# First weight pieces one k-tile at a time, seven warming products, and three reorderings in the DeltaNet stage of a two-layer decoder trunk

## The chip, the cores and the metric

The kernel runs on one core of one Trainium2 chip. The metric is the device time of one execution in microseconds. Engines are named as in the profile: PE is TensorE (PEld its weight loads), DVE is VectorE, ACT is ScalarE, POOL is GpSimd and SP is SyncE, which issues most DMAs.

## The reference, cut to what matters

The computation is a two-layer decoder trunk over 512 positions and a model width of 1024. Layer 0 mixes tokens by a gated DeltaNet with 8 heads of width 128, layer 1 by a Conformer convolution. Both layers then cross-attend into 256 memory rows and apply a squared-ReLU MLP of width 4096.

```python
h = x
for layer in range(DEPTH):
    if layer % N_MIXERS == 0:
        h = h + gated_deltanet(rms_norm(h, dn_norm[j]), dn_w_in[j], ...)
    else:
        h = h + conformer_conv(rms_norm(h, cv_norm[j]), ...)
    h = h + memory_cross_attention(rms_norm(h, xa_norm[layer]), rms_norm(mem, ...), ...)
    h = h + sq_relu_mlp(rms_norm(h, mlp_norm[layer]), mlp_w_up[layer], mlp_w_down[layer])
return rms_norm(h, final_norm)
```

The change lies in the first half of layer 0. There the input is projected to q, k, v, z and to two gate values per head; q, k and v pass a causal convolution of width 4 and a SiLU; and the delta rule is solved in chunks, which needs the inverse of a triangular matrix for each head and chunk:

```python
beta = jax.nn.sigmoid(b_raw)
g = -jnp.exp(a_log) * jax.nn.softplus(a_raw + dt_bias)
...
a_mat = jnp.eye(DN_CHUNK, dtype=q.dtype) + lower
sol = lax.linalg.triangular_solve(a_mat, rhs, left_side=True, lower=True, unit_diagonal=True)
...
return o.astype(h.dtype).reshape(B, S, DN_INNER) @ w_out
```

## The kernel before, in words

**Products.** Each fp32 product is made of three matmuls on split operands: a value is cut into a high part (`wh`, `xh`, an fp32r copy made by ACT) and a low part (`wl`, `xl`, the remainder, made by DVE), and `mm3` (L236 to L240) multiplies high by high, high weights by low input, and low weights by high input into one PSUM bank. Weights come in pieces of 128x1024 (eight k-tiles of 128x128, a "unit" of 24 matmuls): SP loads the raw piece, ACT casts it (`wh`, L214), DVE subtracts (`wl`, L69). Raw pieces, `wh` and `wl` have three buffers each, so that the cast of one unit waits for the end of the unit three before it.

**Order.** The work of the DeltaNet stage is a list `mains` of units of PE (the projections) and a table `S` of side jobs by unit, with ranks; `run` emits them in that order, and a scheduler then lays each engine's instructions out. An engine runs its own instructions strictly one after another. `tc.keep_in_program_order` holds the marked instructions in the order in which they are written.

**The start.** The first unit (`mm_ab`) multiplies the first k weights and, with the same input tiles, the gate columns (`ab`): five matmuls for each of eight k-tiles. For it the kernel loads eight tiles `x` of the input (256 KB each), the norm's gains `gn0`, the gate columns `wab` and the raw weights `raw0` in four pieces of two k-tiles (`piece`, L106). Piece 0 and 1 are issued on ACT's queue, the rest on SP's in the order x0, gn0, wab, x1, x2, piece 2, x3, x4, piece 3, x5 to x7. A loop (L1298 to L1308) splits the pieces and tiles in that order, pinned. Until the data are there, PE multiplies constants: `WARM` products of 128x128 (L125), each two records in the trace.

**The norm's spread.** The RMS norm's factor per token is computed beside the first units; `spread` (L355) makes it a row for all partitions by four PE transposes (`rb`, L308) and a copy on ACT. It stands after the first part of the third unit (`k`, 2), which `halves` cuts after two k-tiles. `gates` (L387) stands inside that unit's second part, after k-tile `CUT_G`: it transposes the gate values (`abT`, L391), and a series of small DVE operations (`sm`) makes `g` and `beta`. From `g` come `grep` (L431), a PE product `ct` (L454), its copy `gsum` on ACT (L456), and on DVE the matrices `R` and `L` (L69, L72), which the PE products `dt` (L475) multiply. PE's products `dt` stand right behind unit (`q`, 1) and three small products `gsum` (L469 to L471).

**The inverse.** `fs_steps` solves 32x32 blocks by 31 steps on DVE; `fs_end` transposes the result to `UB` (L601); `mg_a` (L613) copies the blocks of each head to `u0` (L617, two copies on ACT and two on DVE a head) and transposes it on DVE to `x0` (L619); `mg_w` multiplies `x0` on PE (`mg`, L628), heads 0 and 1 in one place of the order, heads 2 and 3 one unit later.

**The output.** `do_mm` (L1430) multiplies the heads' outputs `oh`, `ol` (made by `head_out`) with the output weights, in `mm3`'s order.

Of the kernel before, what the change touches and what calls it, by code (L numbers as in the profile page):

```python
# [14 lines left out]
P = 128  # L15
# [22 lines left out]
def tile_trunk(ctx, tc, xT, memT, x_d, mem_d, prm_d, adt_d, bdw_d, tap_d, fin_d, w_ab, w_kq, w_v, w_z, w_dno, w_pw1, w_pw2,  # L38
               w_q, w_k, w_vv, w_o, w_up, w_dn, yT):
    nc = tc.nc  # L40
# [64 lines left out]

    def piece(e, i):  # L106
        e.dma_start(out=raw0[:, i * 256:(i + 1) * 256], in_=w_kq[0][:, i * 256:(i + 1) * 256])

    piece(act, 0)
    wab = slot(s="wab")[:, 0:P]  # L110
    def load_first():
        nc.sync.dma_start(out=gn0, in_=prm_d[:, 0:8])
        nc.sync.dma_start(out=wab, in_=w_ab)

    xin = load_x({0: load_first, 2: lambda: piece(nc.sync, 2), 4: lambda: piece(nc.sync, 3)})
    adt = const([P, 16], "adt")

# [6 lines left out]
    for i in range(WARM):  # L124
# [6 lines left out]
                       base=0, channel_multiplier=1)  # L131
    piece(act, 1)
    ones_r = const([P, P], "ones_r", F32R)
# [235 lines left out]
    class DeltaNet:  # L369
# [243 lines left out]
        def mg_a(self, h):  # L613
            (u0, bt), n = self.M[h], slice(h % 4 * 4, h % 4 * 4 + 4)
            for b in range(4):
                bs = slice(32 * b, 32 * b + 32)
                (act.copy if b % 2 else dve.tensor_copy)(c4(u0)[bs, :, bs], self.fs[h // 4][bs, n, :])  # L617
            x0 = slot(s="x0")
            dve.transpose(out=x0, in_=u0)  # L619
            self.M[h] = u0, x0, bt  # L620
# [676 lines left out]
    pin = tc.keep_in_program_order  # L1297
    for i in range(4):  # L1298
        s = slice(i * 256, (i + 1) * 256)
        pin(act.copy(hl0[0][:, s], raw0[:, s]))  # L1300
        pin(tt(dve, hl0[1][:, s], raw0[:, s], hl0[0][:, s].bitcast(F32), ALU.subtract))
        for k in (2 * i, 2 * i + 1):
            n0.parts(k, xin[k], pin)
# [29 lines left out]
    def main(kind, h):  # L1333
        at[kind, h] = len(mains)
        k2 = (kind, h) == ("k", 2)
        mains.extend(halves((kind, h // 2), h % 2, n0.xs, D.ps, (kind, h), 2 if k2 else 4, {CUT_G: D.gates} if k2 else None))

# [92 lines left out]
    def do_mm(q, m):  # L1430
        if m % 2 == 0:
            wdo[0] = wnext(("do", 2 * q + m // 4), m // 2 % 2)
        ps = psum("do")
        for k in range(4):
            mm3(ps, wk(wdo[0], m % 2 * 4 + k), os_[4 * q + k], k == 0, k == 3)
        return ps
# [15 lines left out]
    h = []  # L1452
# [72 lines left out]
LAG = (0, 0, 1)  # L1525
WARM = 9
FENCE = 9
T_STAT = 5
CUT_G = 5
T_DEC = 13  # L1530
# [127 lines left out]
```

## Time and profile before

| what | value |
|---|---|
| median of 3 runs | 1502.61 us (1502.39 to 1503.71) |
| the profiled execution's own time | 1502.59 us |
| its span, first to last instruction | 1500.9 us |
| PE busy | 1492.3 us, 99% of the span |
| DVE, ACT, POOL busy | 894.5, 685.1, 211.7 us |
| granted TensorE clock | 1.0 |

The profiled execution lies 1.7 us above its span and within 0.1 us of the median. The profile's page gives the span, busy time by engine and the chain that ended last. The timeline view lists instructions in order of time: start in us, duration in us, engine, line, operation, output<-inputs, shapes, count, and in square brackets the engine's idle time before it with what ended it. The view of waits sums idle time by what ended it (total, times, longest). The windows view gives each engine's busy time in stretches of time. Matmuls are pipelined: a matmul of 512 columns is shown with 0.39 us, but the next one starts earlier than that.

### The profile page before, as it was taken

The numbers are of one execution on the slowest core, as the hardware profiler recorded it, in microseconds if no ns is written. First come the engines' busy times: TensorE is split into PE (matmuls) and PEld (weight loads), VectorE is DVE, ScalarE is ACT, GpSimd is POOL, SyncE is SP. The second block draws the span as 40 slices with busy tenths as digits, with TensorE's granted clock in tenths as the row PEclk, the third lists the DMA queues.
The fourth block names the chain that finished last, engine by engine and source line by source line (L and its number), as shares of the span: only waits on it lengthen the run. The fifth ranks groups of instructions, "written<-read, shape, count | busy, mean of one in ns | idle before, by whom it ended". The sixth has DMA issues, their size and how long they took to land.

```text
span 1500.9 us, 19206 instructions
## 1 busy us (share of the span) xinstructions
PE 1492.3 (99%) x7458; PEld 1257.9 (84%) x7458; DVE 894.5 (60%) x1318; ACT 685.1 (46%) x1202; POOL 211.7 (14%) x223
## 2 busy tenths in 40 slices
PE   9999999999999999999999999999999999999998
PEld 7888889888888888888888889988888888888886
DVE  6889888867555543444445799976555543434441
ACT  7856765555444432322324464564444431423332
POOL 1401310102111000000002496211111000000000
PEclk9999999999999999999999999999999999999999
DMA  7231223522212222223233624532122223322221
GB/s 250 74 119 57 71 85 113 182 85 88 81 47 95 99 98 98 98 99 97 92 126 128 190 87 138 173 123 98 57 71 91 92 98 98 98 98 99 98 99 56
DMA packets 50059, 155.65 MB, mean 104 GB/s; under 512 B 6320, under 2 KB 8624, under 8 KB 49968
## 3 DMA queue, kind: packets, MB, share of 16 engines
q1 hardware_dynamic: 49536, 153.90, 30.7%
q8 instruction: 58, 0.95, 0.3%
q10 hardware_dynamic: 432, 0.52, 0.1%
q14 instruction: 33, 0.27, 0.1%
HBM read 151.52 MB, written 2.10 MB: 102 GB/s over the span
## 4 chain that ended last, share of the span: by engine, by line
PE 92%; DVE 3%; ACT 2%; issue 1%; DMA 1%; POOL 0%; SPq 0%; DVEq 0%; POOLq 0%
PE up L240 8%; PE up L238 8%; PE up L239 8%; PE dn L240 7%; PE dn L238 7%; PE dn L239 7%; PE pw L240 3%; PE pw L239 3%; PE pw L238 3%; PE h L238 2%; PE h L239 2%; PE h L240 2%; PE xo L239 2%; PE q L238 2%; PE xo L240 2%; PE q L239 2%
## 5 line engine op out<-in xcount | busy, mean ns | idle before, releaser
L214 ACT CAST wh<-raw 128x1024 fp32r<-128x1024 f32 x247 | 259.2, 1051 | 598.0 <-PE dn L239 194.8
L69 DVE TENSOR_TENSOR wl<-raw,wh 128x1024 fp32r<-128x1024 f32 (+1 forms) x238 | 290.0, 1220 | 83.4 <-ACT wh L214 77.1
L240 PE MATMUL up<-xh,wl 128*128 128x512 f32 x512 | 199.2, 389 | 0.0
L239 PE MATMUL up<-xl,wh 128*128 128x512 f32 x512 | 199.2, 389 | 0.0
L238 PE MATMUL up<-xh,wh 128*128 128x512 f32 x512 | 199.2, 389 | 0.0
L240 PE MATMUL dn<-uh,wl 128*128 128x512 f32 x448 | 174.3, 389 | 0.0
L238 PE MATMUL dn<-uh,wh 128*128 128x512 f32 x448 | 174.3, 389 | 0.0
L239 PE MATMUL dn<-ul,wh 128*128 128x512 f32 x448 | 174.3, 389 | 0.0
L69 DVE TENSOR_TENSOR h<-dn,h 128x512 f32<-128x512 f32 x56 | 41.8, 747 | 165.3 <-PE dn L240 165.3
L72 DVE SCALAR_TENSOR_TENSOR rl<-up,rb 128x512 f32<-128x512 f32 x64 | 44.2, 691 | 153.8 <-PE up L240 153.7
L69 POOL TENSOR_TENSOR sq<-sq,sq 128x512 f32<-128x512 f32 x30 | 49.3, 1642 | 486.0 <-ACT sq L331 475.7
L239 PEld LDWEIGHTS up<-xl,wh 128*128 128x128 f32 x512 | 96.1, 188 | 20.0
L240 PEld LDWEIGHTS up<-xh,wl 128*128 128x128 f32 x512 | 96.1, 188 | 20.0
L238 PEld LDWEIGHTS up<-xh,wh 128*128 128x128 f32 x512 | 96.1, 188 | 19.8
L239 PEld LDWEIGHTS dn<-ul,wh 128*128 128x128 f32 x448 | 84.1, 188 | 17.5
L240 PEld LDWEIGHTS dn<-uh,wl 128*128 128x128 f32 x448 | 84.1, 188 | 17.4
L238 PEld LDWEIGHTS dn<-uh,wh 128*128 128x128 f32 x448 | 84.1, 188 | 17.4
L1144 DVE SCALAR_TENSOR_TENSOR ca<-x,prm,ca 128x512 f32<-128x512 f32 x112 | 82.3, 753 | 3.6 <-ACT ca L1141 1.3
L238 PE MATMUL h<-xh,wh 128*128 128x512 f32 x184 | 73.7, 401 | 0.0
L240 PE MATMUL h<-xh,wl 128*128 128x512 f32 x184 | 71.9, 391 | 0.0
L239 PE MATMUL h<-xl,wh 128*128 128x512 f32 x184 | 71.7, 390 | 0.0
L72 DVE SCALAR_TENSOR_TENSOR cva<-cv,prm,cva 128x512 f32<-128x512 f32 x60 | 48.2, 829 | 11.4 <-POOL cva L69 10.3
(362 smaller groups left out, 3036.0 us busy)
## 6 DMA issues: line engine op xcount, KB each, us to landing
raw<-w_up SPq DMA_DIRECT2D x64, 512.0 KB, 3.4
raw<-w_dn SPq DMA_DIRECT2D x64, 512.0 KB, 3.4
raw<-w_pw SPq DMA_DIRECT2D x24, 512.0 KB, 3.6
raw<-w_k SPq DMA_DIRECT2D x16, 512.0 KB, 3.5
raw<-w_vv SPq DMA_DIRECT2D x16, 512.0 KB, 3.6
raw<-w_q SPq DMA_DIRECT2D x16, 512.0 KB, 3.4
raw<-w_o SPq DMA_DIRECT2D x16, 512.0 KB, 3.6
raw<-w_kq SPq DMA_DIRECT2D x15, 512.0 KB, 3.6
```

Of the source, the lines that this page charges most:

```text
L69: return e.tensor_tensor(out=o, in0=a, in1=b, op=op)
L72: return dve.scalar_tensor_tensor(out=o, in0=a, scalar=s, in1=b, op0=op0, op1=op1)
L214: ins = [act.copy(h, raw)]
L238: pe.matmul(ps, wh, xh, start=first, stop=False)
L239: pe.matmul(ps, wh, xl, start=False, stop=False)
L240: pe.matmul(ps, wl, xh, start=False, stop=last)
L1144: first["tap"] = dve.scalar_tensor_tensor(out=a, in0=src, scalar=w, in1=a, op0=ALU.mult, op1=ALU.add)
```

## The change

Five edits, all in the DeltaNet stage.

1. The first weights come in five pieces: k-tiles 0 and 1 alone, then 2-3, 4-5 and 6-7. ACT's queue issues k-tile 0, `gn0` and k-tile 1; SP's issues x0, `wab`, x1, piece 2-3, x2, x3, piece 4-5, x4, x5, piece 6-7, x6, x7. The pinned loop splits in the same steps.
2. `WARM` is 7 in place of 9.
3. Unit (`k`, 2) is cut after four k-tiles, and `CUT_G` is 7: the transposes `rb` and `abT` stand six matmuls later on PE.
4. `mg_a` pins the copies and transposes of heads 0 to 3 in the order in which they are written: two DVE copies, transpose, head by head.
5. `do_mm` multiplies low weights by high input before high weights by low input.

```diff
@@ -103,16 +103,14 @@
 
     raw0 = wp.tile([P, 1024], F32, tag="raw", name="raw0", bufs=NRAW)
 
-    def piece(e, i):
-        e.dma_start(out=raw0[:, i * 256:(i + 1) * 256], in_=w_kq[0][:, i * 256:(i + 1) * 256])
-
-    piece(act, 0)
+    def piece(e, k0, k1):
+        e.dma_start(out=raw0[:, k0 * P:k1 * P], in_=w_kq[0][:, k0 * P:k1 * P])
+
+    piece(act, 0, 1)
+    act.dma_start(out=gn0, in_=prm_d[:, 0:8])
+    piece(act, 1, 2)
     wab = slot(s="wab")[:, 0:P]
-    def load_first():
-        nc.sync.dma_start(out=gn0, in_=prm_d[:, 0:8])
-        nc.sync.dma_start(out=wab, in_=w_ab)
-
-    xin = load_x({0: load_first, 2: lambda: piece(nc.sync, 2), 4: lambda: piece(nc.sync, 3)})
+    xin = load_x({0: lambda: nc.sync.dma_start(out=wab, in_=w_ab), 1: lambda: piece(nc.sync, 2, 4), 3: lambda: piece(nc.sync, 4, 6), 5: lambda: piece(nc.sync, 6, 8)})
     adt = const([P, 16], "adt")
 
 
@@ -129,7 +127,6 @@
     tri_gt = const([P, P], "tri_gt")
     pool.affine_select(out=tri_gt, in_=ones, pattern=[[-1, P]], compare_op=ALU.is_gt, fill=0.0,
                        base=0, channel_multiplier=1)
-    piece(act, 1)
     ones_r = const([P, P], "ones_r", F32R)
     pool.tensor_copy(ones_r, ones)
     tri_mid = const([P, P], "tri_mid")
@@ -614,9 +611,13 @@
             (u0, bt), n = self.M[h], slice(h % 4 * 4, h % 4 * 4 + 4)
             for b in range(4):
                 bs = slice(32 * b, 32 * b + 32)
-                (act.copy if b % 2 else dve.tensor_copy)(c4(u0)[bs, :, bs], self.fs[h // 4][bs, n, :])
+                i = (act.copy if b % 2 else dve.tensor_copy)(c4(u0)[bs, :, bs], self.fs[h // 4][bs, n, :])
+                if h < 4:
+                    tc.keep_in_program_order(i)
             x0 = slot(s="x0")
-            dve.transpose(out=x0, in_=u0)
+            i = dve.transpose(out=x0, in_=u0)
+            if h < 4:
+                tc.keep_in_program_order(i)
             self.M[h] = u0, x0, bt
 
 
@@ -1295,11 +1296,11 @@
     ws["split"], ws["hl"][0] = 1, hl0
     ws["raw"].pop(0)
     pin = tc.keep_in_program_order
-    for i in range(4):
-        s = slice(i * 256, (i + 1) * 256)
+    for k0, k1 in ((0, 1), (1, 2), (2, 4), (4, 6), (6, 8)):
+        s = slice(k0 * P, k1 * P)
         pin(act.copy(hl0[0][:, s], raw0[:, s]))
         pin(tt(dve, hl0[1][:, s], raw0[:, s], hl0[0][:, s].bitcast(F32), ALU.subtract))
-        for k in (2 * i, 2 * i + 1):
+        for k in range(k0, k1):
             n0.parts(k, xin[k], pin)
             if k == 0:
                 wab3 = wab.rearrange("p (k x) -> p k x", k=KT)
@@ -1333,7 +1334,7 @@
     def main(kind, h):
         at[kind, h] = len(mains)
         k2 = (kind, h) == ("k", 2)
-        mains.extend(halves((kind, h // 2), h % 2, n0.xs, D.ps, (kind, h), 2 if k2 else 4, {CUT_G: D.gates} if k2 else None))
+        mains.extend(halves((kind, h // 2), h % 2, n0.xs, D.ps, (kind, h), 4, {CUT_G: D.gates} if k2 else None))
 
     def mm_ab():
         w = wnext(("k", 0), 0)
@@ -1432,7 +1433,10 @@
             wdo[0] = wnext(("do", 2 * q + m // 4), m // 2 % 2)
         ps = psum("do")
         for k in range(4):
-            mm3(ps, wk(wdo[0], m % 2 * 4 + k), os_[4 * q + k], k == 0, k == 3)
+            (wh, wl), (xh, xl) = wk(wdo[0], m % 2 * 4 + k), os_[4 * q + k]
+            pe.matmul(ps, wh, xh, start=k == 0, stop=False)
+            pe.matmul(ps, wl, xh, start=False, stop=False)
+            pe.matmul(ps, wh, xl, start=False, stop=k == 3)
         return ps
 
     def do_first(m):
@@ -1523,10 +1527,10 @@
 PRE = ((2, 4), (2, 6))
 DN_ORDER = (("k", 0), ("q", 0), ("z", 0), ("v", 0), ("k", 1), ("q", 1), ("z", 1), ("v", 1))
 LAG = (0, 0, 1)
-WARM = 9
+WARM = 7
 FENCE = 9
 T_STAT = 5
-CUT_G = 5
+CUT_G = 7
 T_DEC = 13
 NW = 3
 CONV_K, CONV_Q, CONV_V = 0, 1, (1, 1, 0, 0, 1, 1, 0, 0)
```

Since the scheduler lays out each engine anew, other instructions move too. On DVE the series `sm` stands after the transposes `abT`; `cv` is the eviction of unit (`q`, 0) and `wl` the low part of the weights of unit (`q`, 3), which belong to other work. Before:

```order
L72 SCALAR_TENSOR_TENSOR sm_373<-sm_373,sm_371 128x32 x6
L72 SCALAR_TENSOR_TENSOR sm_381<-sm_373,sm_369 128x32
L76 TENSOR_SCALAR sm_383<-sm_355 128x32
L72 SCALAR_TENSOR_TENSOR sm_385<-sm_381,sm_383 128x32
L76 TENSOR_SCALAR sm_390<-sm_361 128x32
L445 TENSOR_REDUCE sm_400<-ident 128x32
L69 TENSOR_TENSOR g<-sm_385,sm_363 128x32
L434 RECIPROCAL beta<-sm_390 128x32
L431 COPY grep_388<-g 128x128
L442 TENSOR_REDUCE ind<-ident 128x4
L446 TENSOR_REDUCE headm<-sm_400 128x8
L69 TENSOR_TENSOR cv_479<-h_454,rb_313 128x512
```

And now, from the second of the seven steps on (line numbers are those of the changed file):

```order
L69 TENSOR_TENSOR cv_480<-h_455,rb_320 128x512
L72 SCALAR_TENSOR_TENSOR sm_380<-sm_380,sm_378 128x32
L69 TENSOR_TENSOR wl_486<-raw_411,wh_485 128x1024
L72 SCALAR_TENSOR_TENSOR sm_380<-sm_380,sm_378 128x32 x3
L72 SCALAR_TENSOR_TENSOR sm_388<-sm_380,sm_376 128x32
L76 TENSOR_SCALAR sm_390<-sm_362 128x32
L72 SCALAR_TENSOR_TENSOR sm_392<-sm_388,sm_390 128x32
L76 TENSOR_SCALAR sm_397<-sm_368 128x32
L442 TENSOR_REDUCE sm_401<-ident 128x32
L69 TENSOR_TENSOR g<-sm_392,sm_370 128x32
L431 RECIPROCAL beta<-sm_397 128x32
L428 COPY grep_395<-g 128x128
```

The eviction `cv` and the weights' `wl` stood behind `headm` and now stand inside the series, ahead of `grep`.

On ACT, in the same stretch, the copy `gsum` of the product `ct` stands among the first convolution taps (`cva`, `cvq`) and the casts of weights (`wh`). Before:

```order
L214 CAST wh_484<-raw_410 128x1024
L492 ACTIVATE cva_508<-cv_479,prm 128x512
L496 ACTIVATE cvq_510<-cv_479,prm 128x512
L456 CAST gsum<-ct_501 128x128
L492 ACTIVATE cva_515<-cv_407,prm 128x512
L492 ACTIVATE cva_520<-cv_445,prm 128x512
L214 CAST wh_582<-raw_448 128x1024
```

And now:

```order
L211 CAST wh_485<-raw_411 128x1024
L453 CAST gsum<-ct_502 128x128
L489 ACTIVATE cva_509<-cv_480,prm 128x512
L493 ACTIVATE cvq_511<-cv_480,prm 128x512
L489 ACTIVATE cva_516<-cv_408,prm 128x512
L489 ACTIVATE cva_521<-cv_446,prm 128x512
L469 ACTIVATE egd<-gsum_538 128x96
```

`gsum` has moved ahead of the two taps' products `cva` and `cvq`, and the cast of the next weights (`wh_582` before) has left this place: it now stands fifteen rows further down, behind the decay's exponentials, a table load, three SiLUs and two more taps. On PE, `ct` stands six matmuls later within unit (`q`, 1), and `dt` where it was. A little earlier on ACT, the cast of the weights of unit (`q`, 1) has moved between the first two products `cva`.

On DVE, the copies `u` and transposes `x` of heads 0 to 3 behind `UB`. Before:

```order
L617 COPY u_214_1064<-UB_1208 32x4x32 x2
L617 COPY u_222_1099<-UB_1208 32x4x32 x2
L619 STREAM_TRANSPOSE x_244_1214<-u_214_1064 128x512
L619 STREAM_TRANSPOSE x_245_1220<-u_222_1099 128x512
L617 COPY u_230_1143<-UB_1208 32x4x32 x2
L617 COPY u_238_1178<-UB_1208 32x4x32
L619 STREAM_TRANSPOSE x_246_1226<-u_230_1143 128x512
L617 COPY u_238_1178<-UB_1208 32x4x32
L69 TENSOR_TENSOR cv_1308<-h_1283,rb_313 128x512
L619 STREAM_TRANSPOSE x_247_1232<-u_238_1178 128x512
```

And now:

```order
L614 COPY u_214_1065<-UB_1209 32x4x32 x2
L618 STREAM_TRANSPOSE x_244_1215<-u_214_1065 128x512
L614 COPY u_222_1100<-UB_1209 32x4x32 x2
L69 TENSOR_TENSOR cv_1309<-h_1284,rb_320 128x512
L618 STREAM_TRANSPOSE x_245_1221<-u_222_1100 128x512
L614 COPY u_230_1144<-UB_1209 32x4x32 x2
L69 TENSOR_TENSOR wl_1321<-raw_1238,wh_1320 128x1024
L618 STREAM_TRANSPOSE x_246_1227<-u_230_1144 128x512
L614 COPY u_238_1179<-UB_1209 32x4x32 x2
L618 STREAM_TRANSPOSE x_247_1233<-u_238_1179 128x512
```

Each transpose now follows its own two copies, the eviction `cv` stands ahead of the second transpose, and the weights' `wl` ahead of the third.

## The prediction

> **What bounds the kernel now.** I read the page first, for the chain that ended last, then who waited for whom on the engine that holds it, then that engine's timeline where it waits.
>
> ```profile
> span 1500.9 us, 19206 instructions
> ...
> PE 92%; DVE 3%; ACT 2%; issue 1%; DMA 1%; POOL 0%; SPq 0%; DVEq 0%; POOLq 0%
> ```
>
> Nine tenths of the chain is PE. The view of waits for PE alone lists no more than this (total, times, longest):
>
> ```profile
> PE warm L125 <- POOL ones L122: 1.2, 1, 1.2
> PE h L1343 <- ACT xh L324: 0.4, 1, 0.4
> PE rb L308 <- DVE rstd L353: 0.3, 1, 0.3
> ```
>
> So PE is idle for 1.9 us in all. It also waits without showing idle time, since a matmul's row reaches past the start of the next; those waits show as steps between starts. A step without a wait comes from the windows view (stretch, its length, then busy time and count of PE, PEld, DVE, ACT and POOL, granted clock, DMA share, GB/s): the second unit, 24 matmuls (x25 counts one that hangs over the edge), fills its stretch exactly, 0.227 us each.
>
> ```profile
> 5.44:15.78 10.34, 10.23 (x40) 5.92 (x41) 8.02 (x13) 7.71 (x13) 0.00 (x0) 1.00 1.02 363
> 15.78:21.22 5.44, 5.44 (x25) 4.50 (x24) 1.38 (x2) 5.03 (x10) 2.07 (x3) 1.00 0.95 366
> ```
>
> The first unit, 40 matmuls, would take 9.07 at that step and takes 10.34: 1.27 us lost. Everything that the change can win lies in the first 5.44 us, in these 1.27, and in three waits of a few tenths priced below; 0.2% of this kernel, about what a measurement can tell from no change, is 3.0 us.
>
> **The first pieces.** The start (timeline of all engines):
>
> ```profile
> 0.80 0.89 ACTq L107 DMA_DIRECT2D raw<-w_kq  x2
> 1.20 3.80 PE L125 MATMUL warm<-ones 128*128 128x128 f32 x18 [1.20 <-POOL ones L122]
> ...
> 2.18 0.91 SPq L98 DMA_DIRECT2D x<-xT  x2
> 4.36 0.40 ACT L1300 CAST wh<-raw 128x256 fp32r<-128x256 f32 x1 [1.36 <-DMA raw<-w_kq]
> 4.67 0.72 ACT L324 ACTIVATE xh<-x,gn 128x512 fp32r<-128x512 f32 x1
> ...
> 5.30 0.28 ACT L1306 CAST abp<-wab 128x128 fp32r<-128x128 f32 x1
> 5.44 0.50 PE L1343 MATMUL h<-xh,wh 128*128 128x512 f32 x1 [0.44 <-ACT xh L324]
> ...
> 6.36 0.72 ACT L324 ACTIVATE xh<-x,gn 128x512 fp32r<-128x512 f32 x1 [0.78 <-DMA x<-xT]
> ...
> 14.71 1.22 DVE L69 TENSOR_TENSOR wl<-raw,wh 128x1024 fp32r<-128x1024 f32 x1 [0.51 <-ACT wh L214]
> ```
>
> PE's first real matmul waits for the input's high part `xh`, and that for the cast of piece 0 on ACT, 0.40. Half of it is one k-tile, for which the 128-column cast of `abp` shows 0.28: 0.12 sooner. The second `xh` waited 0.78 for its tile x1. x1 was SP's fourth issue and becomes the third; an issue takes 0.45 (two in 0.89), so it can be that much sooner. Together 0.57. But the second unit cannot follow: its third matmul needs the `wl` that DVE ends at 14.71+1.22=15.93, so the unit cannot start before 15.93-0.45=15.48, 0.30 ahead of 15.78, unless its raw weights land sooner, and these come behind the same bytes as before. **I take 0.30 won.** The ends: all 1.27 won; or 0.3 lost, if the piece that now stands ahead of x2 delays it by its issue and takes back the rest. In the Trainium skill, "DMA: Bandwidth & Descriptors", section "Issuing engines are not separate DMA queues", speaks against a gain: transfers issued by different engines run on the same 16 DMA engines, and a second issuer saves only the time to issue. By that rule the first term would be nothing and the sum 1503.5; the trace leaves it open, since no row here moves a tile between the issuers.
>
> The two warming products left out are four records of some 0.2; they lie ahead of data that come at 4.36 or later, so they cost nothing by themselves. What their absence may do is a rival below.
>
> **The norm's spread.**
>
> ```profile
> 22.36 0.39 PE L240 MATMUL h<-xh,wl 128*128 128x512 f32 x1
> 23.04 0.62 PE L308 MATMUL rb<-ident,rstd 128*128 128x128 f32 x4 [0.29 <-DVE rstd L353]
> ```
>
> The step is 0.68 instead of 0.227: PE waited 0.45 for `rstd`. Six matmuls later is 1.36 later, and PE being 0.30 ahead still leaves it 0.6 late enough: **0.45 won**, from here on PE is 0.75 ahead. The copy of `rb` on ACT and what DVE does behind it come some 0.6 later, but DVE is held there by a weights' `wl`, so little of it passes on.
>
> **The gates' series, where I see the price.** The series `sm` on DVE, its users on ACT, and PE:
>
> ```profile
> 37.59 1.55 DVE L72 SCALAR_TENSOR_TENSOR sm<-sm,sm 128x32 f32<-128x32 f32 x7
> ...
> 40.01 0.16 DVE L431 COPY grep<-g 128x128 f32<-128x128 f32 x1
> ...
> 41.08 1.23 DVE L69 TENSOR_TENSOR wl<-raw,wh 128x1024 fp32r<-128x1024 f32 x1
> 42.79 0.61 DVE L69 TENSOR_TENSOR gsum<-ct,gsum 32x128 fp32r<-32x128 f32 x2 [0.48 <-ACT gsum L456]
> ...
> 44.63 0.69 DVE L72 SCALAR_TENSOR_TENSOR L<-gsum,headm 64x512 fp32r<-64x512 f32 x1
> ```
> ```profile
> 39.13 1.05 ACT L214 CAST wh<-raw 128x1024 fp32r<-128x1024 f32 x1 [2.63 <-issue]
> ...
> 42.52 0.24 ACT L456 CAST gsum<-ct 128x128 fp32r<-128x128 f32 x1
> ```
> ```profile
> 41.83 0.38 PE L454 MATMUL ct<-tri_mid,grep 128*128 128x128 f32 x2
> ...
> 45.47 1.16 PE L475 MATMUL dt<-R,L 128*128 128x512 f32 x4
> ```
>
> Before, `grep` was ready at 40.17, `ct` ran on PE at 41.83, ACT copied it at 42.52 behind two taps, and `R`, `L` followed; `L` ended at 45.32, `dt` began 0.15 later. So this chain already ended within 0.15 of PE's need. In the new order the eviction `cv` and the weights' `wl` stand inside the series. That `wl` needs its cast, and the cast needs the end of unit (`q`, 0) on PE: 39.13 before, 38.38 with PE 0.75 ahead. The cast ends at 39.43, `wl` at 40.66. Behind it come four of the seven steps and the rest to `grep`: before, from 37.59+3x0.22=38.25 to 40.17, 1.92. So `grep` is ready at 42.58 and `ct` starts at 42.73 (its place on PE: 41.83+1.36-0.75=42.44, so it waits 0.3). ACT no longer has taps ahead of the copy, which comes at 42.73+0.38+0.05=43.16 and not 0.3 after `ct`'s end; from ACT's copy to `dt` it took 45.47-42.52=2.95, so `dt` starts at 46.11. That is 0.64 later than before, though PE came 0.75 ahead: **the edit costs 1.39**. Every step of it is tied to PE's end of unit (`q`, 0), so a larger gain at the start moves it too. The ends: 0, if the scheduler's order is not what binds (PE keeps 0.75), and 2.2, if `wl` waits another 0.8 for a cast delayed on ACT.
>
> **The merges.**
>
> ```profile
> 117.58 1.88 DVE L617 COPY u<-UB 32x128 f32<-32x128 f32 x4
> 119.50 1.30 DVE L619 STREAM_TRANSPOSE x<-u 128x512 f32<-128x512 f32 x2
> ...
> 122.52 0.69 DVE L69 TENSOR_TENSOR cv<-h,rb 128x512 f32<-128x512 f32 x1
> ```
> ```profile
> 119.85 0.39 PE L240 MATMUL h<-xh,wl 128*128 128x512 f32 x1
> 120.36 2.00 PE L628 MATMUL mg<-x,bt 128*128 128x96 f32 x16
> ```
>
> PE was free for `mg` at 119.85+0.23=120.08 and began at 120.36, when the first transpose had ended (119.50+0.65, and 0.21 to PE). Now two copies (0.47 each) stand ahead of it: it ends at 117.58+0.94+0.65=119.17, and 0.28 is won. Head 1, though: two copies to 120.11, the eviction `cv` to 120.80, the transpose to 121.45, on PE by 121.65. Head 0's products take half of 2.00, so PE wants it at 121.08 and waits 0.57. **Net 0.3 lost.** DVE's and PE's shift are the same here, since DVE waited for PE at 94.85 (below). Ends: 0.28 won if `cv` finds no time lost, 0.9 lost if the copies on ACT lag too.
>
> **The output's order.**
>
> ```profile
> 337.64 1.17 PE L238 MATMUL do<-oh,wh 128*128 128x512 f32 x4
> 338.89 0.50 PE L239 MATMUL do<-ol,wh 128*128 128x512 f32 x1
> ```
>
> Four matmuls at 0.227 from 337.64 end their steps at 338.55, and the one on `ol` began at 338.89. With the other product first it is wanted 0.23 later: **0.3 won** of 0.34. Ends: 0 and 0.34. Later rows of `do` show no such step.
>
> **Sum.** -0.30-0.45+1.39+0.3-0.3=+0.64. The profiled execution took 1502.59, which is the median to 0.02; forecast **1503.2**.
>
> **The rivals.** *First, the edits do what they move things for*: the series on DVE does not bind, since its inserted work finds gaps, and head 1 does not wait. Against it: DVE had no gap there except 0.48 before `gsum`. Then -0.30-0.45-0.28-0.3=-1.3: 1501.3. Chance 0.22.
>
> *Second, the array stays at its slow pace longer.*
>
> ```profile
> 4.13 0.87 PE L125 MATMUL warm<-ones 128*128 128x128 f32 x5
> ```
>
> The first 13 records of `warm` take 0.225 each (from 1.20 to 4.13), the last four start within some 0.6: the pace doubles 3.2 us after PE's first product. With four records fewer PE falls idle at that very moment, until about 5.3. If the change of pace then comes a further 3.2 us later, at 7.6, matmuls of the first two k-tiles take twice 0.227; 2.3 us at half pace lose 1.15, of which the waits there hide about half, and as much again if it slips once more: 0.6 to 1.8, I take 1.2, so 1504.4. Chance 0.10. This is the rule of the Trainium skill's "TensorE: Matmul & The Clock Gate", section "What's actually happening": half rate by default, full rate after a busy window of about 3.4 us, and the windows run free of the kernel's start. Nine products (3.8 us) outlast such a window and seven (about 3.1) don't; the trace's 3.2 is in line with it.
>
> *Third, slower by DVE's arrears.* The z weights' first cast moved down ACT's order behind the SiLUs.
>
> ```profile
> 45.35 5.48 DVE L72 SCALAR_TENSOR_TENSOR cva<-cv,prm,cva 128x512 f32<-128x512 f32 x7
> ...
> 55.77 0.75 DVE L72 SCALAR_TENSOR_TENSOR cva<-cv,prm,cva 128x512 f32<-128x512 f32 x1 [0.98 <-POOL cva L69]
> ```
> ```profile
> 54.43 1.30 POOL L69 TENSOR_TENSOR cva<-cva,cvq 128x512 f32<-128x512 f32 x1 [1.82 <-ACT cvq L496]
> ```
> ```profile
> 94.85 0.69 DVE L69 TENSOR_TENSOR cv<-h,rb 128x512 f32<-128x512 f32 x1 [2.39 <-PE h L240]
> ```
>
> From `L`'s end at 45.96 DVE does `cv` and eight taps of 0.78, to 52.9, and then waits for POOL's sum of two taps that ACT makes only after its SiLUs: it ended at 54.43+1.30=55.73, and with `dt` 0.64 later it ends at about 56.3, an idle 3.4 where it was 0.98. These 2.4 us are just what DVE later has to spare where it waits for PE, 2.4 at 94.85. My forecast counts them as hidden. From 3.0 us of arrears on (2.4 and PE's own 0.64) each further one passes to `mg` in full. A second hole like it gives 2x2.4-3.0=1.8 more: 1505.0, slower than before. Chance 0.13.
>
> **How the numbers follow.** Forecast 0.55 for 1503.2, with its own ends at about 1502.3 and 1504.1; rivals 0.22, 0.10, 0.13. The range runs from the first rival to the third, 1501.2 to 1505.0; some 0.2 is left outside. Faster by over 0.2% (under 1499.6) would need more than all the waits named: 0.04. Slower by over 0.2% (over 1505.6) needs the third rival with more arrears, or the second twice: 0.11. Within 0.2%: 0.85.
>
> **What would show it.** In the changed profile: the first real matmul near 5.3; the second unit's start near 15.5; no step before `rb`; `ct` near 42.7, `dt` near 46.1 with a wait of over 1 us behind the products `gsum`; a wait of half a microsecond between the `mg` of heads 0 and 1; no step at the first `ol`. I am wrong if `dt` follows without a wait, if the second `h` unit is at half pace, or if DVE's wait for PE near 95 is gone.

## The result and the profile after

The changed kernel takes 1505.64 us (median of 16 runs, 1504.80 to 1506.46), the kernel before 1502.62 (16 runs, 1502.14 to 1503.71). The ratio is 1.002 with a 95% interval of 1.0012 to 1.0027: 3.0 us or 0.2% slower. The forecast was 1503.2 with a range of 1501.2 to 1505.0; the time lies above it. The changed kernel's profiled execution took 1505.43, with a span of 1503.7 where it was 1500.9.

In the changed kernel, the view of waits for PE (total, times, longest) has two entries that the kernel before had not, `dt` and `G`, and a third, `mg`, that was forecast. The wait for `rstd` is gone:

```profile
PE dt L472 <- DVE L L72: 1.7, 1, 1.7
PE warm L123 <- POOL ones L120: 1.2, 1, 1.2
PE h L1344 <- ACT xh L321: 1.0, 1, 1.0
PE G L526 <- ACT kt L530: 0.6, 1, 0.6
PE mg L629 <- DVE x L618: 0.4, 1, 0.4
```

The timeline of PE shows where each stands (start, duration, operation, idle time before it):

```profile
24.30 0.60 PE L305 MATMUL rb<-ident,rstd 128*128 128x128 f32 x4
...
43.29 0.46 PE L451 MATMUL ct<-tri_mid,grep 128*128 128x128 f32 x2
...
45.33 0.39 PE L468 MATMUL gsum<-g,tri_le 128*128 128x32 f32 x2
47.40 0.93 PE L472 MATMUL dt<-R,L 128*128 128x512 f32 x3 [1.67 <-DVE L L72]
...
70.94 1.16 PE L526 MATMUL G<-cva 128*128 128x128 f32 x8 [0.60 <-ACT kt L530]
...
122.83 1.02 PE L629 MATMUL mg<-x,bt 128*128 128x96 f32 x8
124.26 1.13 PE L629 MATMUL mg<-x,bt 128*128 128x96 f32 x8 [0.41 <-DVE x L618]
...
338.93 2.21 PE L781 MATMUL ogT<-ident,z 128*128 128x128 f32 x16
```

The way to read two such traces is to set the same PE instruction of both side by side: the difference of the starts, as it grows from one place to the next, is what each place costs. At `rb` and `ct` the six matmuls that were moved (1.36) have to be taken off.

| place on PE | before | after | cost or gain of the place | forecast |
|---|---|---|---|---|
| second unit | 15.78 | 16.14 | +0.36 | -0.30 |
| `rb`, the wait for `rstd` | 23.04 | 24.30 | -0.46 | -0.45 |
| `dt` | 45.47 | 47.40 | +2.03 | +1.39 |
| `G` of the fourth head | 68.26 | 70.94 | +0.84 | 0 |
| `mg` of head 0 | 120.36 | 122.83 | -0.30 | -0.28 |
| `mg` of head 1 | inside the group | 124.26 | +0.49 | +0.57 |
| output, `ogT` to `do` | 335.90 | 338.93 | -0.1 | -0.3 |
| sum | | | +2.9 | +0.64 |

(The place of `G` counts what PE has lost when its second product begins, 2.77, less the 1.93 at `dt`.) Behind the second unit, no other place moves PE by more than a tenth.

**The wait for `dt`.** On DVE in the changed kernel, the row that stands out is `L`, 1.81 us where the same operation took 0.69:

```profile
42.98 0.16 DVE L428 COPY grep<-g 128x128 f32<-128x128 f32 x1
...
44.08 0.61 DVE L69 TENSOR_TENSOR gsum<-ct,gsum 32x128 fp32r<-32x128 f32 x2 [0.55 <-ACT gsum L453]
44.72 0.69 DVE L69 TENSOR_TENSOR R<-gsum,ind 64x512 fp32r<-64x512 f32 x1
45.44 1.81 DVE L72 SCALAR_TENSOR_TENSOR L<-gsum,headm 64x512 fp32r<-64x512 f32 x1
```

POOL and ACT at that time, changed kernel (POOL's sum of two convolution taps, and the taps on ACT behind the copy `gsum`):

```profile
45.43 1.26 POOL L69 TENSOR_TENSOR cva<-cva,cvq 128x512 f32<-128x512 f32 x1 [0.60 <-ACT cvq L493]
```
```profile
43.79 0.27 ACT L453 CAST gsum<-ct 128x128 fp32r<-128x128 f32 x1 [3.73 <-PE ct L451]
43.95 0.73 ACT L489 ACTIVATE cva<-cv,prm 128x512 f32<-128x512 f32 x1
44.57 0.71 ACT L493 ACTIVATE cvq<-cv,prm 128x512 f32<-128x512 f32 x1
```

POOL's sum starts with `L` and ends at 46.69; `L` ends 0.56 later, at 47.25, though it has only 0.69 of work: it did not run beside the sum. The kernel before had the same pair one operation sooner, POOL and then DVE:

```profile
42.76 1.29 POOL L69 TENSOR_TENSOR cva<-cva,cvq 128x512 f32<-128x512 f32 x1
```
```profile
43.43 1.17 DVE L69 TENSOR_TENSOR R<-gsum,ind 64x512 fp32r<-64x512 f32 x1
```

There the sum ended at 44.05 and `R`, caught halfway, at 44.60, 0.55 later. So the collision cost 0.48 before (1.17 against 0.69) and costs 1.12 now. It moved because ACT's copy `gsum` now stands ahead of the two taps that the sum adds, so that the sum starts just as `L` does. The Trainium skill has this rule in "SBUF — State Buffer", section "SBUF: two separate sides": DVE and GpSimd share a pair of ports, which is a lock and not a split; a DVE operation with two SBUF inputs and a GpSimd operation that reads SBUF exclude each other for a whole instruction, whichever came first. The trace agrees: 1.81 against 0.69.

**The wait for `G`.** ACT ahead of it in the changed kernel:

```profile
68.03 1.76 ACT L576 COPY DB<-bt 32x128 f32<-32x128 f32 x4
69.81 0.60 ACT L528 ACTIVATE sqk<-kt 128x512 f32<-128x512 f32 x1
70.30 0.58 ACT L530 COPY kt<-kt 128x512 f32<-128x512 f32 x1
```

The fourth head's `G` needs a PSUM buffer, and in the new order it is given the one that ACT's copy `kt` of the head before empties. That copy stands behind four copies `DB`. In the kernel before, the same matmul, at 68.26, waited for a release by DVE instead, which came in time: it has no idle time before it. Nothing in the edits names `G`: when the order of the work shifted, the buffers were dealt out in another order too. This reading is tested below, with `G` ahead of the transposes.

### The profile page after: what moved, and what is told of

The parts are those of the page before. It is cut to its first block, busy times and chain, and to the rows that moved or that the text cites. A ratio compares the mean times of both kernels' runs of the same rounds, so it can differ in the third digit from the quotient of the medians.

```text
span 1503.7 us, 19196 instructions
## 1 busy us (share of the span) xinstructions
PE 1492.3 (99%) x7454; PEld 1257.4 (84%) x7454; DVE 895.0 (60%) x1319; ACT 685.1 (46%) x1203; POOL 211.6 (14%) x223
## 4 chain that ended last, share of the span: by engine, by line
PE 77%; DVE 0%; POOL 0%; issue 0%; ACT 0%; DVEq 0%
PE up L236 8%; PE up L235 8%; PE up L237 8%; PE dn L235 7%; PE dn L236 7%; PE dn L237 7%; PE pw L235 3%; PE pw L237 3%; PE pw L236 3%; PE xo L236 2%; PE q L235 2%; PE xo L235 2%; PE q L236 2%; PE q L237 2%; PE xo L237 2%; PE cv L1208 1%
## 5 line engine op out<-in xcount | busy, mean ns | idle before, releaser
L69 DVE TENSOR_TENSOR wl<-raw,wh 128x1024 fp32r<-128x1024 f32 (+2 forms) x239 | 290.7, 1218 | 84.0 <-ACT wh L211 77.9
L69 DVE TENSOR_TENSOR h<-dn,h 128x512 f32<-128x512 f32 x56 | 41.8, 746 | 165.4 <-PE dn L237 165.4
L69 POOL TENSOR_TENSOR sq<-sq,sq 128x512 f32<-128x512 f32 x30 | 49.3, 1643 | 485.8 <-ACT sq L328 475.6
```

Source lines behind the costliest of these rows:

```text
L69: return e.tensor_tensor(out=o, in0=a, in1=b, op=op)
```

## The experiments

Theory A: edit 3 (the spread six matmuls further down) carries the whole loss, by what it does to the order on DVE and ACT. Rivals are named where an experiment tells them apart.

### Edit 3 undone

```diff
-        mains.extend(halves((kind, h // 2), h % 2, n0.xs, D.ps, (kind, h), 4, {CUT_G: D.gates} if k2 else None))
+        mains.extend(halves((kind, h // 2), h % 2, n0.xs, D.ps, (kind, h), 2 if k2 else 4, {CUT_G: D.gates} if k2 else None))
...
-CUT_G = 7
+CUT_G = 5
```

> The changed kernel with its third edit taken back: unit (k, 2) cut after two k-tiles, CUT_G 5. Theory A (the later norm and gates cost the time: in the changed kernel dt came 2.0 us later against PE's work and G another 0.8): the waits of 1.7 before dt and 0.6 before G are gone, the wait before rb is back (0.45 lost again), the start stays 0.36 late, the merges cost some 0.2 and the output gains 0.1: about 0.4 above the kernel before, so near 1503.0, span near 1501.4. Rival (the start's delay is what makes the later stages late): dt or G still wait, and the time stays above 1504.5.

Measured: 1503.29 (11 runs, 1502.94 to 1504.05) beside 1502.87 for the kernel before, ratio 1.0003 (0.9994 to 1.0012). `dt` and `G` wait no longer. Edit 3, which by itself wins 0.46 at `rb`, brings the loss.

### Edit 3 kept, the series kept together

The two operations that had slipped into the series, the eviction `cv` of (`q`, 0) and the `wl` of (`q`, 3), are issued behind `grep`:

```diff
-        ins.append(tt(pool if gp else dve, lo, raw, h.bitcast(F32), ALU.subtract))
+        with tc.issue_after(ws["grep"].ins) if u == 7 else nullcontext():
+            ins.append(tt(pool if gp else dve, lo, raw, h.bitcast(F32), ALU.subtract))
...
-            dve.tensor_copy(self.grep.rearrange("p (a x) -> p a x", a=4), over_c(g))
+            ws["grep"] = dve.tensor_copy(self.grep.rearrange("p (a x) -> p a x", a=4), over_c(g))
...
-            self.M["q", h] = self.conv_raw(self.ps.pop(("q", h)))
+            with tc.issue_after(ws["grep"].ins) if h == 0 else nullcontext():
+                self.M["q", h] = self.conv_raw(self.ps.pop(("q", h)))
```

> The changed kernel with the eviction cv of unit (q, 0) and the wl of unit (q, 3) held behind grep on DVE, so that the gates' series stands as before, only six matmuls later in its start; ct goes back to its old place on PE by itself. Theory A (what stands inside the series costs the time): grep ready near 40.4, ct not waiting, dt within 0.6 of its place on PE, no wait before G: 0.0 to 0.6 above the kernel before, 1502.6 to 1503.2. Rival B (the transposes abT six matmuls later make the series late by themselves): dt still waits over 1.2 and the time stays above 1504. Rival C (POOL's sum of two taps holds the matrix L): L takes 1.8 again, and dt waits by that, 0.6, whatever the series does.

Measured: 1503.45 (1502.65 to 1504.17), ratio 1.0004 (0.9995 to 1.0013). `grep` starts 2.6 us sooner (40.36 against 42.98), and `G` waits no longer. DVE and POOL of this kernel:

```profile
44.05 1.76 DVE L72 SCALAR_TENSOR_TENSOR L<-gsum,headm 64x512 fp32r<-64x512 f32 x1
```
```profile
43.96 1.29 POOL L69 TENSOR_TENSOR cva<-cva,cvq 128x512 f32<-128x512 f32 x1 [0.84 <-ACT cvq L494]
```

The series is cured and `dt` still waits 0.3, since `L` still meets POOL's sum: two causes, one behind the other.

### Edit 3 kept, series together, no sum on POOL there

Beside the last kernel, head 0's q taps go to DVE alone:

```diff
-            self.M["q", h] = self.conv_taps(self.M["q", h], h, CONV_Q)
+            self.M["q", h] = self.conv_taps(self.M["q", h], h, CONV_Q if h else 0)
```

> The changed kernel with the series held together as in the second experiment, and besides with head 0's q convolution without the tap that ACT multiplies and POOL adds (DVE takes that tap, 0.75). Theory A (DVE's L took 1.76 there because POOL's sum ran beside it from 43.96 to 45.25): L takes 0.69, ends near 44.7, and dt runs at its place on PE without a wait, so PE is 0.5 ahead of the second experiment from there on: span near 1501.0, time near 1502.9. Rival (L is slow by its own operands, a strided read of gsum): L takes 1.7 again and dt comes at the same place as there.

Measured: a median of 1506.90 (1504.59 to 1507.45), ratio 1.0022 (1.0013 to 1.0031). Its profile has `L` at 0.69 and `dt` at 45.14 without a wait, as expected, so the collision is what stretched `L`. But another product waits in its place, since DVE has the tap now:

```profile
70.05 1.16 PE L528 MATMUL G<-cva 128*128 128x128 f32 x8 [1.93 <-DVE dt L69]
```

The expected time was missed, and `G` is again the reason; by the trace it waits here for DVE's `dt` (L69), so for a buffer that DVE empties. The runs fall into two groups, 1504.6 to 1505.0 and 1506.6 to 1507.5, of which more below.

### Before, with edit 3, and POOL's sum held behind `L`

The kernel before, edits 3 and 5, the series kept together as above, and a copy on POOL of one column of `L`, for which POOL's sum has to wait:

```diff
-                    tt(pool, a, a, b, ALU.add)
+                    c = pool.tensor_copy(small(1), self.L[0][:, 0:1].bitcast(F32)) if ti == 0 else None
+                    with tc.issue_after(c.ins) if c else nullcontext():
+                        tt(pool, a, a, b, ALU.add)
```

> The kernel before with the third and fifth edit, the series held together on DVE (cv and wl behind grep), and on POOL one small copy of a column of L ahead of the sum of head 0's two q taps, so that POOL's sum starts behind L (the copy's result is not used). Theory A (the port that POOL's sum and DVE's L share is what held L and dt; the series and the buffer of G were the other two): L takes 0.69 and dt runs at its place, G does not wait, the wait before rb is gone: 0.45 won there and 0.1 at the output, span near 1500.3, time near 1502.2, the first version below the kernel before. Rival (POOL's sum, now beside the taps, delays DVE and comes back at G or mg): a wait at G of the fourth head or at mg, time 1502.8 or more.

Measured: 1502.13 (11 runs, 1501.94 to 1502.78) beside 1502.96, ratio 0.9994 (0.9985 to 1.0003); its span is 1500.4. DVE, POOL and PE's only wait in this kernel:

```profile
43.65 0.69 DVE L72 SCALAR_TENSOR_TENSOR L<-gsum,headm 64x512 fp32r<-64x512 f32 x1
```
```profile
44.51 0.66 POOL L498 COPY sm<-L 128x1 f32<-128x1 f32 x1 [1.78 <-DVE L L72]
45.13 1.29 POOL L69 TENSOR_TENSOR cva<-cva,cvq 128x512 f32<-128x512 f32 x1
```
```profile
PE warm L125 <- POOL ones L122: 1.2, 1, 1.2
```

With both side effects taken out, edit 3 gives at `rb` what it was forecast to give (0.45 here, 0.46 in the changed kernel), and `dt` and `G` follow without a wait. Its median is under both kernels', though the interval reaches 1.0003.

### The Gram product ahead of the transposes

To try the buffer's story by itself, the fourth head's `G` is issued ahead of its `kt` in the changed kernel, so that `kt` takes the late buffer:

```diff
+            if h == 3:
+                psg = psum("G")
+                for c in range(4):
+                    cs = slice(c * P, (c + 1) * P)
+                    pe.matmul(psg[:, cs], kT[:, cs], kT[:, cs], start=True, stop=True)
...
-            psg = psum("G")
-            for c in range(4):
-                cs = slice(c * P, (c + 1) * P)
-                pe.matmul(psg[:, cs], kT[:, cs], kT[:, cs], start=True, stop=True)
+            if h != 3:
+                psg = psum("G")
+                for c in range(4):
+                    cs = slice(c * P, (c + 1) * P)
+                    pe.matmul(psg[:, cs], kT[:, cs], kT[:, cs], start=True, stop=True)
```

> The changed kernel with the products G of head 3 put ahead of its transposes kt, so that G takes the other buffer of the pair. Theory A (G waits 0.6 in the changed kernel only because its PSUM buffer is the one that ACT's copy of the head before, kt, reads, and that copy stands behind four copies DB; in the kernel before G had a buffer that DVE had long left): G runs without a wait, and kt, which now takes that buffer, waits some 0.3; PE is 0.4 to 0.5 ahead of the changed kernel from there on, span near 1503.3. Rival (G waits because ACT and DVE are behind with the input of that head): the first of the two waits as before, no gain, span 1503.7.

PE of this kernel:

```profile
70.34 1.05 PE L524 MATMUL G<-cva 128*128 128x128 f32 x8
71.51 0.66 PE L527 MATMUL kt<-ident,cva 128*128 128x128 f32 x4
```

`G` does not wait and `kt` only a little: from `dt` on PE loses 0.33 more here, where the changed kernel lost 0.84. So `G` had waited for the buffer and not for its input. The median is 1505.63 (1505.17 to 1507.36), ratio 1.002 (1.0011 to 1.0029), no lower than the changed kernel's: the half microsecond is in the trace and not in the times. For the profiled execution the reason is its start, with a second unit at 16.72 instead of 16.14; for the median it stays open.

### Edits 4 and 5 alone

The kernel before, with the pinned merges and the output's order, as in the diff of the change.

> The kernel before with the fourth and fifth edit alone (merges head by head, the output's order). Theory A: mg of head 0 starts 0.28 sooner, head 1 then waits some 0.5 behind the eviction cv, together 0.2 lost; at the output the step before the first ol goes (0.34) and 0.23 comes back at the transposes ogT ahead of it: 0.1 above the kernel before, 1502.7, span 1501.0. Rival (in the kernel before, DVE is not late at the merges, and head 1 does not wait): span 1500.4, some 0.4 below.

Measured: 1503.12 (1502.11 to 1503.87), ratio 1.0001 (0.9993 to 1.001). PE of this kernel at the merges:

```profile
119.71 1.02 PE L632 MATMUL mg<-x,bt 128*128 128x96 f32 x8
121.16 1.13 PE L632 MATMUL mg<-x,bt 128*128 128x96 f32 x8 [0.42 <-DVE x L621]
```

Head 0 gains 0.25, head 1 loses 0.50; at the output the second `ogT` comes 0.23 later and the step at `ol` is gone, which wins 0.1: together 0.1 to 0.2 lost, nothing that a time could show. This is the merges' step as forecast.

### The pieces' bytes and the warming products

First, pieces of k-tiles 2-5 and 6-7 in place of 2-3, 4-5 and 6-7, so that the same number of transfers as before stands ahead of the input tiles:

```diff
-    xin = load_x({0: lambda: nc.sync.dma_start(out=wab, in_=w_ab), 1: lambda: piece(nc.sync, 2, 4), 3: lambda: piece(nc.sync, 4, 6), 5: lambda: piece(nc.sync, 6, 8)})
+    xin = load_x({0: lambda: nc.sync.dma_start(out=wab, in_=w_ab), 1: lambda: piece(nc.sync, 2, 6), 5: lambda: piece(nc.sync, 6, 8)})
...
-    for k0, k1 in ((0, 1), (1, 2), (2, 4), (4, 6), (6, 8)):
+    for k0, k1 in ((0, 1), (1, 2), (2, 6), (6, 8)):
```

> The changed kernel with k-tiles 2 to 5 of the first weights in one piece behind x1 and 6-7 behind x5, so that the first eight transfers carry the bytes that they carried before (in the changed kernel they carry 128 KB fewer). Theory A (only eight transfers are open at a time; the ninth waits for the first to land, and with less in the first eight the DMA engines run dry for 128 KB / 363 GB/s = 0.36 us): the stream has no hole before x3, x7 lands near 12.3 and not 12.7, the second unit starts near 15.8 and not 16.1, all 0.36 sooner: about 1505.3. Rival (x4 is late because a further piece stands ahead of it): x2 and x3 come later than now, x7 still lands near 12.7 and the second unit starts near 16.1.

Measured: 1506.10 (1505.08 to 1506.56), ratio 1.0019 (1.0011 to 1.0028). The tile x4 landed at 9.06 instead of 10.29, but the second unit began at 16.98, because PE kept its half pace (0.43 a matmul, as against 0.227) until 10.3. Inconclusive on the transfers, and no gain.

Then `WARM` 9 and `WARM` 5 in the changed kernel:

```diff
-WARM = 7
+WARM = 9
```

> The changed kernel with nine warming products and nothing else. Theory A (the granted clock rises at the end of some window of a few us that is busy enough; the gap of 1.1 to 1.3 behind seven products spoils that window in about half of the executions, and the first ten matmuls then run at half the pace, as in the profiles of the first and third experiment, where the clock rose at 9.6 and 10.2 and the second unit came 0.5 to 0.8 later than in the changed kernel's own profile): the times near 1506.2, half of those of the changed kernel, are gone, the median is near 1505.2, the clock rises before 7.2 in the profile. Rival (the moment of the rise is chance and does not depend on these products): median 1505.6 and as wide a scatter.

Measured: 1505.89 (1505.04 to 1506.41), ratio 1.002 (1.0011 to 1.0029). The expectation failed: the times are no lower and no narrower.

```diff
-WARM = 7
+WARM = 5
```

> The changed kernel with five warming products, which end near 3.4, so that PE stands idle for 2 us. Theory A (as for nine): nearly every execution has the late rise, between 8 and 11 us, the second unit starts near 16.9, the median is near 1506.2, with few times near 1505.2. Rival (chance): median 1505.6.

Measured: 1506.57 (1505.51 to 1507.68), ratio 1.0025 (1.0016 to 1.0033); with nine products on the same chip it was 1505.89. In this profile PE is at half pace until 10.7 and the second unit begins at 17.19. So fewer products do keep the array slow for longer. Over all profiles: with nine, full pace had come by 7.1 at the latest (seven profiles); with seven it came by 5.2 in three and at 9.7, 10.3 and 9.7 in three. Those three began the second unit at 16.7 to 17.0, those with an early rise and the new pieces at 15.5 to 16.3, and those with the old pieces at 15.5 to 16.4.

### The start as before

Edits 1 and 2 undone, edits 3 to 5 kept:

```diff
-    for k0, k1 in ((0, 1), (1, 2), (2, 4), (4, 6), (6, 8)):
+    for i in range(4):
...
-WARM = 7
+WARM = 9
```

> The changed kernel with the first two edits taken back (the first weights' pieces and the order of the first loads as before, nine warming products). Theory A (the new order of the first loads costs 0.36 to 0.7 at the second unit, and the rest of the loss, dt, G and merges, follows PE unchanged): dt waits 1.7, G 0.6, second unit near 15.7, span near 1503.3, median near 1505.1. Rival (the start's lateness makes part of the waits at dt and G, since ACT's cast and DVE's series follow the end of unit (q, 0)): these waits are shorter and the median is below 1504.5.

Measured: 1505.96 (1504.87 to 1506.98), ratio 1.002 (1.0011 to 1.0029). Undoing the start wins nothing. Its profiled execution (1506.52) caught what the changed kernel's had not. PE of this kernel at `dt`:

```profile
45.60 0.39 PE L471 MATMUL gsum<-g,tri_le 128*128 128x32 f32 x2
47.65 1.79 PE L475 MATMUL dt<-R,L 128*128 128x512 f32 x4 [1.67 <-DVE L L72]
49.24 0.63 PE L238 MATMUL h<-xh,wh 128*128 128x512 f32 x1
49.66 0.63 PE L239 MATMUL h<-xl,wh 128*128 128x512 f32 x1
...
50.95 0.59 PE L239 MATMUL h<-xl,wh 128*128 128x512 f32 x1
51.37 0.40 PE L240 MATMUL h<-xh,wl 128*128 128x512 f32 x1
51.61 0.40 PE L238 MATMUL h<-xh,wh 128*128 128x512 f32 x1
```

and a row of the windows view of the same kernel (the last three numbers: granted clock, DMA share, GB/s):

```profile
49.24:51.37 2.13, 2.13 (x6) 1.65 (x5) 2.13 (x4) 2.13 (x6) 1.50 (x3) 0.50 0.04 8
```

Behind the wait the matmuls step by 0.43 and the granted clock is 0.50, until 51.4. Between 47.9 and 51.4 the loss is 1.6 against the changed kernel's profile, of which 0.74 comes back, since PE then is late enough not to wait for `G`. Of the 11 runs, the seven from 1505.92 up have a mean clock of 0.998 and the four others 0.999; 3.4 us at half clock are 0.0011 of 1500. With nine warming products in the changed kernel it was the same: the six runs from 1505.89 up have 0.998, the five below 0.999. No profile without the fall has a mean clock under 0.999, and the two that show it, this one and the one with products behind `dt` below, have 0.998. So in about half of the executions the clock falls, by the profiles behind the wait for `dt`. (The two groups of the kernel without POOL's sum, above, may be of the same kind, behind its wait of 1.93 for `G`: five of the seven upper runs have 0.998, none of the four lower ones. Its profile is of a lower run, so this is not shown.)

### The wait filled, and the same work behind it

If the idle time is what lowers the clock, then less of it should leave the clock alone. Three products of constants stand between `gsum` and `dt`, with `WARM` 9:

```diff
+                for _ in range(3):
+                    pe.matmul(ps_g[:, 256:384], ones, ones, start=True, stop=True)
                 act.activation(self.egd, ps_g[:, 0:96], AF.Exp)
```

> The changed kernel with nine warming products and, between the products gsum and dt, three products of constants (128x128, result not used) that fill 0.67 of the 1.95 us in which PE stands idle before dt; dt itself waits as long as before. Theory A (an idle time of 1.95 lets the granted clock fall to a half for 3.4 us in about half of the executions, as the tenth experiment's profile shows at 47.95; this, not the start, parts the times near 1506.3 from those near 1505.3): with 1.28 idle the clock does not fall, no run has a mean clock of 0.998, all times lie between 1504.9 and 1505.9, median near 1505.3. Rival (the scatter comes from the start or from chance): six of eleven near 1506.3 as with nine warming products alone, median 1505.9.

The rival: the three products matter by themselves, wherever they stand. Here they stand behind `dt`:

```diff
+                if h == 3:
+                    for _ in range(3):
+                        pe.matmul(ps_g[:, 256:384], ones, ones, start=True, stop=True)
```

> The same three products of constants behind dt in place of ahead of it, so that the idle time of 1.95 stays. Theory A: the clock still falls in about half of the executions; PE has 0.67 more work there, which G's wait of 0.6 takes back in part: median near 1506, and a group 0.8 to 1.2 above the other. Rival (the added products steady the clock or the order by themselves, wherever they stand): one narrow group as in the eleventh experiment.

PE of the first:

```profile
45.28 0.91 PE L470 MATMUL gsum<-ones 128*128 128x128 f32 x6
47.12 1.17 PE L474 MATMUL dt<-R,L 128*128 128x512 f32 x4 [0.93 <-DVE L L72]
48.13 0.39 PE L235 MATMUL h<-xh,wh 128*128 128x512 f32 x1
```

and of the second, the granted clock in the windows view:

```profile
47.96:51.37 3.41, 3.41 (x13) 2.92 (x12) 3.41 (x5) 3.41 (x8) 2.04 (x4) 0.50 0.02 5
```

Measured: with the wait filled 1505.26 in one narrow group (1504.89 to 1505.55, none at 0.998), ratio 1.0015 (1.0006 to 1.0023); with the products behind `dt` 1506.61 (1505.47 to 1507.13), ratio 1.0021 (1.0012 to 1.003), six of eleven at 0.998 and 1506.6 or more, five at 1505.5 to 1505.9. The same products at the same count: only where they shorten the idle time do they keep the clock up. Against the changed kernel with nine warming products (1505.89) that is 0.6 of the median.

## Why the prediction was wrong, point by point

The time lies above the range because three terms of the sum were wrong in the same direction: the start, taken as 0.30 won, lost 0.36; the delay of `dt`, taken as 1.39, was 2.03; and `G`, which lost 0.84, was taken as nothing, without a reason given.

- **The first pieces** (forecast 0.30 won): not won. The second input tile came sooner in most profiles, but the second unit began at 16.14. The forecast took the landing of this unit's raw weights as it was, since "these come behind the same bytes as before". ACT's cast of them, which waits for that landing, started 0.37 later, and the unit 0.36 later, some 2.15 behind the cast in both kernels:

```profile
13.62 1.05 ACT L214 CAST wh<-raw 128x1024 fp32r<-128x1024 f32 x1 [0.34 <-DMA raw<-w_kq]
```
```profile
13.99 1.05 ACT L211 CAST wh<-raw 128x1024 fp32r<-128x1024 f32 x1 [0.56 <-DMA raw<-w_kq]
```

With the old pieces this cast started at 13.21 to 14.28 in four profiles, and the unit at 15.53 to 16.36; with the new ones and an early full pace at 13.56 to 14.46 in six. So the 0.36 is within the scatter, and undoing edits 1 and 2 gave nothing.
- **The norm's spread** (0.45 won): right, 0.46.
- **The gates' series** (1.39 lost): the mechanism was right, and the step that failed is its size, "the edit costs 1.39": it cost 2.03. `grep` came at 43.14 instead of 42.58, because PE ended unit (`q`, 0) later than if the start had won (ACT's cast behind it started at 39.01 instead of 38.38, and the `wl` inside the series followed):

```profile
39.01 1.05 ACT L211 CAST wh<-raw 128x1024 fp32r<-128x1024 f32 x1 [2.62 <-issue]
```
```profile
40.09 1.23 DVE L69 TENSOR_TENSOR wl<-raw,wh 128x1024 fp32r<-128x1024 f32 x1
```

That alone moves PE and `dt` together and costs nothing more. But from ACT's copy to `dt` the forecast carried over the 2.95 of before, and it took 3.61: `L` 1.12 longer and `R` 0.48 shorter. The 2.95 already held one collision, `R` at 1.17, which was not looked into; and the forecast noted that the taps moved behind `gsum` without asking where the sum made of them would then fall.
- **`G`** (not in the sum): the term that was missing, 0.84, the largest of the three misses. The order on ACT was shown to have changed, and no buffer was followed through it.
- **The merges** (net 0.3 lost): right in mechanism and place, 0.19.
- **The output** (0.3 won): 0.1. The step at `ol` went, but the second `ogT` came 0.23 later; what holds it was not tried.
- **First rival** (no loss at all): refuted by the changed kernel's profile, where `dt` waits 1.67 and head 1's `mg` 0.41, and by the first experiment, where the loss goes with edit 3. **Second rival** (slow pace for longer): it occurs, in three of six profiles with seven products, where the second unit comes 0.55 to 0.84 later than in the changed kernel's own; this is the lower end of its 0.6 to 1.8. But the changed kernel's own profile has full pace from 4.5, and nine products did not lower the median. **Third rival** (DVE's arrears): the hole came as worked out, 3.31 us on DVE, and DVE's later wait for PE hid it, 0.98 being left of 2.39:

```profile
58.08 0.75 DVE L72 SCALAR_TENSOR_TENSOR cva<-cv,prm,cva 128x512 f32<-128x512 f32 x1 [3.31 <-POOL cva L69]
...
97.60 0.69 DVE L69 TENSOR_TENSOR cv<-h,rb 128x512 f32<-128x512 f32 x1 [0.98 <-PE h L237]
```

The misses add up: 0.66 at the start, 0.64 at `dt`, 0.84 at `G`, -0.1 at `mg`, 0.2 at the output, 2.2 in all, from 1503.2 to the profiled 1505.43. Why the median is a further 0.2 higher is not shown. The 16 runs fall into nine up to 1505.64 and seven from 1505.99 up, and the profiled one is of the lower group. Two things found above could part them: the clock that falls behind the wait, as in the kernels with nine warming products, and the late full pace at the start, as in three of six profiles with seven. Six of the seven upper runs have a mean clock of 0.999, where the runs with the fall had 0.998, and the late pace leaves the mean clock at 0.999 (its three profiles); this speaks for the start, but no profile caught an upper run.

## What to carry to other kernels

When an order moves by a few instructions, follow three things through it, not one: the chain that was moved, every operation on another engine that held up an operation of that chain before and may now fall elsewhere on it (here POOL's sum), and the PSUM buffers that are dealt out anew behind it. A chain that ended within 0.15 us of its consumer, as here, has no room for any of them. Before moving work away from a wait of 0.4 us, look whether what slips into its place can be pinned: with two pins and one small copy edit 3 cost nothing here.

## What the runs showed of the hardware

- **An idle gap of 1.7 us can lower the clock.** PE shows 1.67 us of idle time before `dt`; in 6 or 7 of 11 executions the mean clock is lower by what such a fall takes, and the two profiles that caught it show a clock of 0.5 for 3.41 us. With the gap cut to 0.93 none of 11 runs showed it. The Trainium skill, "TensorE: Matmul & The Clock Gate", section "What's actually happening", has the clock fall after an idle window of about 3.4 us, on windows that run free of the kernel. The 3.41 us and the chance of one half agree with free-running windows; that the whole window must be idle does not agree with the trace. In these two profiles full pace had come at 6.99 and 7.00, and the clock fell at 47.95 and 47.96, twelve times 3.41 later. Counted in such steps from the full pace (an estimate), the gap lies whole inside one step in these two, and is split between two steps in four other profiles with the same gap, which have no fall; but in the changed kernel's own profile it also lies whole inside one, and the clock did not fall. So the gap alone does not decide it, and what does was not tried.
- **A stopped DVE operation ended 0.55 us after POOL's, in three cases.** `R` before and `L` after ended 0.55 and 0.56 after the sum's end, though the one had begun 0.67 and the other 0.01 after the sum's start; with the series kept together it was 0.56 (45.81 against 45.25). Alone, each takes 0.69.
- **The start scatters more than its edits.** The same old pieces gave a second unit at 15.53, 15.78, 15.93 and 16.36 in four profiles; the cast of its weights started at 13.21, 13.62, 13.72 and 14.28 there, in the same order.
